# Eight of 18 pairs by seven products in the second pass of the last product, held transposes, and five rooms for the gate2 loads

## The chip, the cores and the metric

The kernel runs on one core of a Trainium2 chip. The core has engines that run side by side, each through its own instructions in a fixed order: TensorE (PE) multiplies matrices into PSUM banks, VectorE (DVE) and ScalarE (ACT) work element by element, GpSimd (POOL) does little here, and SyncE (SP) issues the transfers (DMA) from the chip's memory. An instruction waits until what it reads is written and what it overwrites has been read, and everything behind it on its engine waits with it. The metric is the time of one execution on the device, in microseconds (us).

## The reference, cut to what matters

One layer of a decoder on 256 rows of width 2048: a modulated norm, three token mixers in parallel (stick-breaking attention, dilated attention, gated linear attention) between one input product and one output product, then a modulated norm and a gated feed-forward network of width 5632.

```python
mod = jax.nn.silu(c) @ w_ada[l] + b_ada[l]
shift1, scale1, gate1, shift2, scale2, gate2 = jnp.split(mod[:, None, :], N_MOD, axis=-1)
h = rms_norm(x, norm1_gain[l]) * (1 + scale1) + shift1
x = x + gate1 * mixing_sublayer(h, w_in[l], ...)
h = rms_norm(x, norm2_gain[l]) * (1 + scale2) + shift2
gate, up = jnp.split(h @ w_ffn_in, 2, axis=-1)
x = x + gate2 * ((jax.nn.silu(gate) * up) @ w_ffn_out)
```

Everything is float32. In the mixers, queries and keys are normalised head by head before the attentions.

## The kernel before, in words

**Products.** Rows lie in two tiles of 128 (t = 0, 1), weights come in loads of two chunks of 128 rows by 512 columns (512 KB, the tile `raw`, issued by SP: L146 in `load_weights`, L1293 in `load_pair`). Each load is split into a high and a low part: ACT casts it (`whi`, L158 and L1305) and DVE subtracts (`wlo`, L159 and L1306). There are four buffers of each. A product is three matmuls of 512 columns (`mm3`, L164 to L166): high by high, high by low, low by high. `block` runs the plain loop over the chunks; at given steps it calls other work, and a small counter (`tick`) hands out background work at a set rate.

**Seven products for eight.** `fast_products` multiplies a pair of chunks by a pair of column blocks and a pair of row tiles. A plain pair takes 8 products, 24 matmuls. A fast pair takes 7 products, 21 matmuls, on sums of the weights' quarters (four DVE subtractions of 128x512, L1309, and two further splits from the tiles `AR0` and `AR1`) and on sums of the activations' quarters made beforehand (`sums_of_h2`, `sums_of_unit`). Four extra banks collect shared products, which DVE merges after the last fast pair (L1381 to L1384, L1340). `load_pair` is called three pairs ahead where there are hooks, for all pairs at once where there are none; its instructions have priority for the scheduler that orders each engine.

**The feed-forward part.** The input product runs over 11 units of 512 columns; units 1 to 7 by fast pairs, units 8 to 10 plainly. Each unit's activation (hi, lo) stays in SBUF as four chunks, 44 in all, which are 22 pairs for the last product: unit e holds pairs 2e and 2e+1. The last product makes output blocks 0 and 1 in a first pass over all 22 pairs (`OUT_A`, 6 fast) and blocks 2 and 3 in a second pass over the first 14 pairs (`OUT_B`, 6 fast: 8 to 13, from units 4, 5 and 6); the other 8 pairs are then done for block 2 (a `block` over chunks 28 to 43) and for block 3 (28 and 29 with both row tiles, the rest first for row tile 0, then for row tile 1, with weights of the last 14 chunks kept, three pairs of loads of them in the tiles H2 to H7). `add_out` multiplies by gate2, adds to x2 and stores (L1447, L1449).

**Sums for the last product.** `sums_of_unit` adds hi and lo (L1462), makes four sums (L1269), casts (L1466) and subtracts (L1467). It is hooked to pairs 2, 4 and 6 of OUT_A; its results stay in H2 to H7.

**gate2.** While units 8 to 10 run, 32 loads of w_ada (512 KB each, L384) come into a ring of three tiles, `AR0`, `AR1`, `KC`, and DVE accumulates them into `ada` (L289). The loads stand on SP's queue among the weight loads. After OUT_A's fast pairs, `parts_of_gate2` and `rows_of_gate2` turn the sums into rows with a few matmuls.

**x2.** The four blocks of the first residual (A2, A3, A4, A8) are put away in memory during the feed-forward part, where their tiles serve as further rooms for split weights in units 1 to 7, and brought back (`bring_back`) by hooks at pairs 8 to 11 of OUT_A.

**Mixers.** After the input blocks 0 to 5, `qk_turn(sb_parts, ...)` transposes normalised queries and keys of the stick-breaking heads with PE (L658) into `misc` banks, and ACT copies them back scaled (L659), which frees the bank. `gla()` follows with 32 small matmuls (L734, L738) and then its own blocks, with steps of the stick-breaking attention among them. For the dilated heads, `qk_norm` squares (L638, ACT), takes a reciprocal root (L269 to L277, DVE and ACT) and multiplies (L646, DVE); `dil_steps` then puts two turns and two halves of the scores (L882, L883) at steps 4, 7, 10 and 13 of the second row block. The softmax across groups uses L898 to L924 (L906 is its Exp on ACT), and PE transposes the weights at L936. The gate blocks copy their result out (L1054), and the sigmoids of the gates come at L1071 and L1074.

**Order.** No order is written out by hand. A scheduler orders each engine's instructions by priority and by readiness in its own model; `prio()` raises priority, and `issue_after` holds an instruction behind a given matmul. A change in one place therefore can move instructions in others.

Of the kernel before, what the change touches and what calls it, by code (L numbers as in the profile page):

```python
# [11 lines left out]
F32R = mybir.dt.float32r  # L12
# [5 lines left out]
P = 128  # L18
T = 256
NT = T // P  # L20
D = 2048
KC = D // P
DFF = 5632
NB = 512
# [20 lines left out]
FAST = range(1, 8)  # L45
OUT_UNITS = (4, 5, 6)
OUT_A = tuple((p, 0) for p in range(8)) + tuple(x for i in range(6) for x in ((8 + i, 1), (14 + i, 0))) + ((20, 0), (21, 0))
OUT_B = ((0, 0), (1, 0)) + tuple(x for i in range(6) for x in ((8 + i, 1), (2 + i, 0)))
PAIRS = ((0, 0), (1, 0), (5, 1), (2, 0), (6, 1), (7, 1), (3, 0), (4, 0))
# [26 lines left out]
def trunk(ctx: ExitStack, tc: tile.TileContext, I, out):  # L76
# [16 lines left out]
    def S(tag, shape, dtype=F32):  # L93
        return slot.tile(shape, dtype, tag=tag, name=nm(tag))
# [22 lines left out]
    state = {"rate": 0.0}  # L117
# [358 lines left out]
    LAST = len(GROUPS) - 1  # L476
# [245 lines left out]
    def gla():  # L722
# [21 lines left out]
        for i, b in enumerate((9, 10, 11, 12)):  # L744
            proj_block(LAST, b, steps={1: lambda: sb_step(2 * i), 3: lambda: sb_step(2 * i + 1)})
        with tc.issue_after(state["mm"].ins), prio():
# [268 lines left out]
    proj_block(LAST, 5)  # L1015
    qk_turn(sb_parts, state["mm"].ins)
    sb_hi, sb_lo, sb_step = stick_breaking()
    og = gla()
    for b in range(6, 9):
# [7 lines left out]
    dil_steps = {  # L1027
        4: lambda: qk_turn(dil_parts[:2]),
        7: lambda: qk_turn(dil_parts[2:]),
        10: lambda: dil_scores(0, 3),  # L1030
        13: lambda: dil_scores(3, 6),
    }
# [185 lines left out]

    def bring_back(n):
        x2[n] = S(X2_TAGS[n], [P, NT, NB])  # L1220
        nc.sync.dma_start(x2[n], x2_away[n])
# [176 lines left out]
    for i in range(NFF):  # L1398
        if i in FAST:
            pg, pu = fast_unit(i)  # L1400
        else:
            pg = [acc_bank() for _ in range(NT)]
        if i == FAST[-1] + 1:
            bg.append(gate2_bg())
        if i in FAST:
# [47 lines left out]
    KF = 4 * NFF  # L1453
    CUT = KF - 14
    w_fo = I["w_ffn_out"]
    out_sums = {}

    def sums_of_unit(n):

        e = OUT_UNITS[n]  # L1460
        full = S("AR0", [P, 4, T])
        nc.vector.tensor_tensor(full, act[e][0].bitcast(F32), act[e][1].bitcast(F32), op=ALU.add)  # L1462
        sf = S("AR1", [P, 4, 2, P])
        sums_of(sf, [full[:, :, t * P : (t + 1) * P] for t in range(NT)], slice(0, 4, 2), slice(1, 4, 2))
        hi, lo = (S(f"H{2 + 2 * n + i}", [P, 4, 2, P], F32R) for i in range(2))
        nc.scalar.copy(hi, sf)  # L1466
        nc.vector.tensor_tensor(lo, sf, hi.bitcast(F32), op=ALU.subtract)  # L1467
        for m in range(2):
            out_sums[2 * e + m] = [(hi[:, j, m, :], lo[:, j, m, :]) for j in range(4)]
# [26 lines left out]

    for n in range(4):
        hooks[8 + n] = lambda n=n: bring_back(n)
    behind = 1 + max(n for n, (_, fast) in enumerate(OUT_A) if fast)
    assert behind + 2 < len(OUT_A)  # L1500
    hooks[behind] = lambda: parts_of_gate2(0)
    hooks[behind + 1] = lambda: both(0)
    hooks[behind + 2] = lambda: rows_of_gate2(1)
    o = fast_products(w_fo, 0, NB, OUT_A, act_at, out_sums, acc_bank, misc_bank, ("AR0", "AR1"), hooks)
# [5 lines left out]
    o = fast_products(w_fo, 2 * NB, 3 * NB, OUT_B, act_at, out_sums, misc_bank, acc_bank, ("AR0", "AR1"), more=True)  # L1510
    REST = 2 * len(OUT_B)
    block(o[0], act_at, w_fo, REST, KF, 2 * NB, go_on=True, seeded=True)
# [4 lines left out]
    n, pss = 3, o[1]  # L1517
    block(pss, act_at, w_fo, REST, CUT, n * NB, go_on=True, more=True, seeded=True)
    w = load_weights(w_fo, CUT, KF, n * NB, spare=[f"H{j}" for j in range(2, 8)])
    block(pss, act_at, None, CUT, KF, 0, w=w, tiles=(0,), go_on=True, seeded=True)  # L1520
# [40 lines left out]
```

## Time and profile before

| | us |
|---|---|
| median of three runs | 1593.85 |
| the three runs | 1590.32, 1593.85, 1594.32 |
| the profiled execution | 1593.15 |
| its span | 1591.4 |
| last matmul starts | 1587.0 |
| PE busy | 1576.3 |
| DVE busy | 1299.3 |
| ACT busy | 850.2 |
| bytes moved by DMA | 400.16 MB |

The span is the time between the first and the last recorded instruction; the execution's own time is 1.75 us longer. A row of a timeline has the start, the duration, engine, line, operation, output and input, and in square brackets how long the engine stood idle before it and what ended that wait. Matmuls are pipelined: each lasts longer than the distance to the next start, so gaps of PE are seen in the starts. Times in the kernel's lines are those of the kernel before; the changed kernel's lines are up to four higher.

### The profile page before, as it was taken

What the parts mean: (1) busy time and instruction counts of PE and PEld (TensorE: products, weight loads), DVE (VectorE), ACT (ScalarE), POOL (GpSimd) and SP (SyncE); (2) the same over time, 40 slices, a digit from 0 to 9 for tenths busy, and PEclk for the clock granted to TensorE, in tenths of its full rate; (3) what the DMA queues carried; (4) which work ended last, traced back from release to release, by engine and by line L of the source; (5) the groups of instructions that cost most, each with busy time, mean ns of one, the idle gap of its engine ahead of it and who ended that gap; (6) DMA issues with size and microseconds to landing.
All of it is one profiled execution on the core that took longest, in us unless ns stands there. A gap on an engine that the chain in (4) does not pass through costs nothing.

```text
span 1591.4 us, 20176 instructions
## 1 busy us (share of the span) xinstructions
PE 1576.3 (99%) x7243; PEld 1304.6 (82%) x7243; DVE 1299.3 (82%) x1556; ACT 850.2 (53%) x1193; POOL 11.2 (1%) x22
## 2 busy tenths in 40 slices
PE   8999999999999999999999999999999999999998
PEld 7878888888788888888887888888888888888887
DVE  6889996888888686877756689999997777989884
ACT  5654448775755444444445755555554444455552
POOL 1000000000000000000000000000000000000000
PEclk9999999999999999999999999999999999999999
DMA  9999997667788899988767556666668889756664
GB/s 330 357 331 322 332 305 235 220 193 248 233 273 271 297 306 316 317 283 293 230 210 240 179 185 196 194 202 196 211 189 276 283 294 313 244 185 218 205 206 139
DMA packets 195740, 400.16 MB, mean 251 GB/s; under 512 B 13038, under 2 KB 28052, under 8 KB 195640
## 3 DMA queue, kind: packets, MB, share of 16 engines
q1 hardware_dynamic: 194664, 396.70, 75.6%
q0 software_dynamic: 800, 2.11, 0.3%
q8 instruction: 57, 0.93, 0.3%
q14 instruction: 43, 0.35, 0.1%
q10 hardware_dynamic: 176, 0.07, 0.0%
HBM read 394.63 MB, written 4.19 MB: 251 GB/s over the span
## 4 chain that ended last, share of the span: by engine, by line
PE 86%; DMA 5%; DVE 5%; ACT 3%; issue 1%; SPq 0%; ACTq 0%; DVEq 0%
PE acc L166 21%; PE acc L165 21%; PE acc L164 21%; PE misc L165 6%; PE misc L166 6%; PE misc L164 6%; DMA raw<-w_ffn_out 1%; DMA AR<-w_ada 1%; DVE ada L289 1%; ACT whi L158 1%; DVE wlo L159 1%; PE misc L809 1%; DMA A<-w_ada 1%; DMA OS<-w_ada 1%; DVE wlo L1306 1%
## 5 line engine op out<-in xcount | busy, mean ns | idle before, releaser
L158 ACT CAST whi<-raw 128x1024 fp32r<-128x1024 f32 x362 | 368.6, 1022 | 411.0 <-PE acc L166 257.2
L159 DVE TENSOR_TENSOR wlo<-raw,whi 128x1024 fp32r<-128x1024 f32 x362 | 426.2, 1184 | 181.3 <-ACT whi L158 179.0
L164 PE MATMUL acc<-whi,H 128*128 128x512 f32 x1245 | 487.3, 392 | 1.4 <-ACT H L455 0.8
L165 PE MATMUL acc<-wlo,H 128*128 128x512 f32 x1245 | 486.5, 391 | 0.8 <-DVE wlo L159 0.7
L166 PE MATMUL acc<-whi,H 128*128 128x512 f32 x1245 | 485.2, 390 | 0.4 <-DVE H L462 0.4
L166 PEld LDWEIGHTS acc<-whi,H 128*128 128x128 f32 x1245 | 233.5, 188 | 50.6 <-DVE H L462 1.6
L164 PEld LDWEIGHTS acc<-whi,H 128*128 128x128 f32 x1245 | 233.7, 188 | 50.2 <-ACT H L455 1.3
L165 PEld LDWEIGHTS acc<-wlo,H 128*128 128x128 f32 x1245 | 233.8, 188 | 48.7 <-DVE wlo L159 1.7
L1305 ACT CAST whi<-raw 128x1024 fp32r<-128x1024 f32 (+1 forms) x148 | 141.9, 974 | 99.8 <-PE acc L166 40.1
L1306 DVE TENSOR_TENSOR wlo<-raw,whi 128x1024 fp32r<-128x1024 f32 (+1 forms) x148 | 162.6, 1122 | 8.1 <-ACT whi L1305 6.8
L164 PE MATMUL acc<-whi,A 128*128 128x512 f32 x222 | 87.0, 392 | 1.0 <-DVE scr L1429 1.0
L165 PE MATMUL acc<-wlo,A 128*128 128x512 f32 x222 | 86.4, 389 | 0.0
L166 PE MATMUL acc<-whi,A 128*128 128x512 f32 x216 | 84.1, 389 | 0.0
L289 DVE SCALAR_TENSOR_TENSOR ada<-AR,csil,ada 128x1024 f32<-128x1024 f32 x60 | 76.1, 1280 | 7.3 <-DMA AR<-w_ada 7.3
L165 PE MATMUL misc<-wlo,H 128*128 128x512 f32 x158 | 61.7, 390 | 0.8 <-DVE wlo L1306 0.8
L164 PE MATMUL misc<-whi,H 128*128 128x512 f32 x158 | 61.7, 391 | 0.0
L166 PE MATMUL misc<-whi,H 128*128 128x512 f32 x158 | 61.5, 389 | 0.0
L164 PEld LDWEIGHTS acc<-whi,A 128*128 128x128 f32 x222 | 41.7, 188 | 9.8 <-issue 1.4
L165 PEld LDWEIGHTS acc<-wlo,A 128*128 128x128 f32 x222 | 41.7, 188 | 8.6 <-DVE wlo L159 0.2
L1305 ACT CAST whi<-AR 128x1024 fp32r<-128x1024 f32 x24 | 25.3, 1053 | 43.6 <-PE acc L166 21.1
L1305 ACT CAST A<-raw 128x1024 fp32r<-128x1024 f32 (+1 forms) x36 | 34.9, 982 | 25.0 <-PE misc L166 8.6
L166 PEld LDWEIGHTS acc<-whi,A 128*128 128x128 f32 x216 | 40.5, 188 | 8.5
(485 smaller groups left out, 2291.0 us busy)
## 6 DMA issues: line engine op xcount, KB each, us to landing
raw<-w_in SPq DMA_DIRECT2D x205, 512.0 KB, 5.2
raw<-w_ffn_in SPq DMA_DIRECT2D x176, 512.0 KB, 4.5
raw<-w_ffn_out SPq DMA_DIRECT2D x88, 512.0 KB, 4.9
AR<-w_ada SPq DMA_DIRECT2D x79, 512.0 KB, 5.0
raw<-w_out SPq DMA_DIRECT2D x32, 512.0 KB, 4.9
KC<-w_ada SPq DMA_DIRECT2D x30, 512.0 KB, 5.2
OS<-w_ada SPq DMA_DIRECT2D x16, 512.0 KB, 6.9
KD<-w_ada SPq DMA_DIRECT2D x16, 512.0 KB, 5.5
```

Of the source, the lines that this page charges most:

```text
L158: state["cast"] = nc.scalar.copy(hi[:, :n, :], raw[:, :n, :])
L159: state["split"] = nc.vector.tensor_tensor(lo[:, :n, :], raw[:, :n, :], hi[:, :n, :].bitcast(F32), op=ALU.subtract)
L164: nc.tensor.matmul(ps, lh, rh, start=start, stop=False, skip_group_check=seeded)
L165: nc.tensor.matmul(ps, lh, rl, start=False, stop=False, skip_group_check=seeded)
L166: state["mm"] = nc.tensor.matmul(ps, ll, rh, start=False, stop=stop, skip_group_check=seeded)
L289: nc.vector.scalar_tensor_tensor(acc, raw, c, acc, op0=ALU.mult, op1=ALU.add)
L809: nc.tensor.matmul(ps[:n, t * N_GLA + h, :].rearrange("p (s l) -> p s l", l=L), at(f, h, t)[:, :n], odd(at(f, h, t)), start=True, stop=True,)
L1305: nc.scalar.copy(hi[:, :n, :], src)
L1306: state["split"] = nc.vector.tensor_tensor(lo[:, :n, :], src, hi[:, :n, :].bitcast(F32), op=ALU.subtract)
```

## The change

The second pass goes over 18 pairs instead of 14, eight of them fast: pairs 6 and 7 (unit 3) join, and a fourth call of `sums_of_unit` makes their sums into A4 and A8, hooked to the pair behind the second `rows_of_gate2`. The rest of block 2 is then 8 chunks instead of 16. Block 3's rest is the same 8 chunks, all of them kept for the second row tile, without the spare rooms H2 to H7. The ring of gate2 gets A2 and A3 as fourth and fifth tiles from unit 8 on. Two blocks of x2 come back in OUT_A as before, the other two after OUT_B's code, into H2 and H3. In the mixers, the first two stick-breaking parts are turned where all four were, and the other two at step 2 of the first block inside `gla`. The dilated turns and scores move from steps 4, 7, 10, 13 to 7, 10, 13, 15, and the turns are held behind the matmul before their step.

```diff
-OUT_UNITS = (4, 5, 6)
+OUT_UNITS = (4, 5, 6, 3)
-OUT_B = ((0, 0), (1, 0)) + tuple(x for i in range(6) for x in ((8 + i, 1), (2 + i, 0)))
+OUT_B = ((0, 0), (1, 0)) + tuple(x for a, b in zip((8, 9, 10, 11, 12, 13, 6, 7), (2, 3, 4, 5, 14, 15, 16, 17)) for x in ((a, 1), (b, 0)))
...
-            proj_block(LAST, b, steps={1: lambda: sb_step(2 * i), 3: lambda: sb_step(2 * i + 1)})
+            steps = {1: lambda: sb_step(2 * i), 3: lambda: sb_step(2 * i + 1)}
+            if i == 0:
+                steps[2] = lambda: qk_turn(sb_parts[2:], state["mm"].ins)
+            proj_block(LAST, b, steps=steps)
...
-    qk_turn(sb_parts, state["mm"].ins)
+    qk_turn(sb_parts[:2], state["mm"].ins)
...
-        4: lambda: qk_turn(dil_parts[:2]),
-        7: lambda: qk_turn(dil_parts[2:]),
-        10: lambda: dil_scores(0, 3),
-        13: lambda: dil_scores(3, 6),
+        7: lambda: qk_turn(dil_parts[:2], state["mm"].ins),
+        10: lambda: qk_turn(dil_parts[2:], state["mm"].ins),
+        13: lambda: dil_scores(0, 3),
+        15: lambda: dil_scores(3, 6),
...
-    def bring_back(n):
-        x2[n] = S(X2_TAGS[n], [P, NT, NB])
+    def bring_back(n, tag):
+        x2[n] = S(tag, [P, NT, NB])
...
         if i == FAST[-1] + 1:
+            ring["tags"] = ("AR0", "AR1", "KC", "A2", "A3")
             bg.append(gate2_bg())
...
-    CUT = KF - 14
+    CUT = 2 * len(OUT_B)
...
-        hi, lo = (S(f"H{2 + 2 * n + i}", [P, 4, 2, P], F32R) for i in range(2))
+        hi, lo = (S(tag, [P, 4, 2, P], F32R) for tag in (("H2", "H3"), ("H4", "H5"), ("H6", "H7"), ("A4", "A8"))[n])
...
-    for n in range(4):
-        hooks[8 + n] = lambda n=n: bring_back(n)
+    for n in range(2):
+        hooks[8 + n] = lambda n=n: bring_back(n, X2_TAGS[n])
...
-    hooks[behind + 2] = lambda: rows_of_gate2(1)
+    hooks[behind + 2] = lambda: (rows_of_gate2(1), sums_of_unit(3))
...
     o = fast_products(w_fo, 2 * NB, 3 * NB, OUT_B, act_at, out_sums, misc_bank, acc_bank, ("AR0", "AR1"), more=True)
-    REST = 2 * len(OUT_B)
+    for n in (2, 3):
+        bring_back(n, f"H{n}")
+    REST = CUT
...
-    block(pss, act_at, w_fo, REST, CUT, n * NB, go_on=True, more=True, seeded=True)
-    w = load_weights(w_fo, CUT, KF, n * NB, spare=[f"H{j}" for j in range(2, 8)])
+    w = load_weights(w_fo, CUT, KF, n * NB)
```

## The prediction, made before the changed kernel was run

> **What bounds the kernel now.** I read the profile from its summary inwards: busy time, then PE's total of waits, then the pace of PE in quiet stretches, then a timeline around each gap.
>
> ```profile
> span 1591.4 us, 20176 instructions
> PE 1576.3 (99%) x7243; PEld 1304.6 (82%) x7243; DVE 1299.3 (82%) x1556; ACT 850.2 (53%) x1193; POOL 11.2 (1%) x22
> ...
> L158 ACT CAST whi<-raw 128x1024 fp32r<-128x1024 f32 x362 | 368.6, 1022 | 411.0 <-PE acc L166 257.2
> ```
>
> The only engine without room is PE. ACT's casts wait mostly for PE to free a buffer (257.2 of 411.0 us), not for data. So two things shorten the run: fewer matmuls, or fewer gaps between them. A window in a quiet stretch (busy time and count by engine, granted clock, DMA share, GB/s) gives the pace:
>
> ```profile
> 1160.00:1200.00 40.00, 40.00 (x182) 33.21 (x181) 37.31 (x47) 22.08 (x26) 0.00 (x0) 1.00 0.65 205
> ```
>
> With the clock at 1.00, matmuls of 512 columns start every 0.2267 us (40 us hold some 176 of them and a few shorter ones; 1352.67 and 1352.90 below are two such starts). "Excess" below means a start-to-start distance less its normal one. The list of PE's waits (in all, times, longest) names the longest two that bear on this change:
>
> ```profile
> PE misc L658 <- DVE A L646: 1.8, 2, 1.1
> PE acc L164 <- DVE scr L1429: 1.0, 1, 1.0
> ```
>
> With those that the timelines below show, the gaps that this change can remove add up to some 5.5 us of 1591.
>
> **Fewer matmuls.** In OUT_B a fast pair and a plain pair are 21 + 24 matmuls. Two more fast pairs take 3 each from the program, and the instruction orders agree: PE has 7077 instructions before and 7071 after. 6 x 0.2267 = **-1.36 us**, if DVE and ACT can feed it. The steady cycle in OUT_B:
>
> ```profile
> 1498.55 0.68 DVE L1309 TENSOR_TENSOR AR<-raw,raw 128x512 f32<-128x512 f32 x1
> ...
> 1503.97 1.22 DVE L1306 TENSOR_TENSOR wlo<-AR,whi 128x1024 fp32r<-128x1024 f32 x1 [1.07 <-ACT whi L1305]
> ...
> 1508.75 0.69 DVE L1309 TENSOR_TENSOR AR<-raw,raw 128x512 f32<-128x512 f32 x1
> ```
>
> One cycle is 10.20 us, 45 matmuls, and DVE idles 1.07 of it waiting for a cast that itself waits for a freed buffer. Two more such cycles therefore run at PE's pace. The start of OUT_B is another matter: the sums of a fourth unit (L1462, four L1269, L1467) now stand in DVE's order between the split of the first fast pair's half tile and its subtractions. Groups between 1352 and 1400 us give their price:
>
> ```profile
> L1467 DVE TENSOR_TENSOR H<-AR,H 128x1024 fp32r<-128x1024 f32 x3 | 3.7, 1217 | 0.0
> L1269 DVE TENSOR_TENSOR AR<-AR,AR 128x256 f32<-128x256 f32 x6 | 2.5, 419 | 0.1
> ...
> L1462 DVE TENSOR_TENSOR AR<-A,T 128x1024 f32<-128x1024 f32 x1 | 1.2, 1216 | 0.0
> ```
>
> 1.22 + 4 x 0.42 + 1.22 = 4.1 us, a little less when the four overlap. Before, this is where DVE stood:
>
> ```profile
> 1474.39 2.36 DVE L1306 TENSOR_TENSOR wlo<-raw,whi 128x1024 fp32r<-128x1024 f32 x2
> ...
> 1478.47 1.42 DVE L1309 TENSOR_TENSOR AR<-raw,AR 128x512 f32<-128x512 f32 x2
> 1481.14 1.22 DVE L1306 TENSOR_TENSOR wlo<-AR,whi 128x1024 fp32r<-128x1024 f32 x1 [1.26 <-ACT whi L1305]
> ```
>
> Stepping DVE on from 1476.7 with these durations, the second split of a sum ends at 1486.7; PE, counted on at 0.2267, wants it at 1486.4. I take **+0.4 us** (with 0.1 for the semaphore), between 0 (DVE's order finishes earlier) and 1.5 (the whole 4.1 less the two idle times of 1.26 per pair). The next pair starts with DVE about level, and 1.07 us of idle per cycle takes up the rest. The last blocks lose their six spare rooms: counting on from the last OUT_B matmul, the four loads of block 3 can start 1 us before to 4.4 us after it, their last split waits for DVE's additions of block 2 and ends 14.5 us after it, and PE wants it at 15.2: no gap.
>
> **Gate2 loads.** Their ring grows from three rooms to five from unit 8 on, and x2 comes back later, two of four blocks in OUT_B. The gap they caused:
>
> ```profile
> 1348.32 1.22 DVE L1306 TENSOR_TENSOR wlo<-raw,whi 128x1024 fp32r<-128x1024 f32 x1
> 1351.08 1.29 DVE L289 SCALAR_TENSOR_TENSOR ada<-AR,csil,ada 128x1024 f32<-128x1024 f32 x1 [1.54 <-DMA AR<-w_ada]
> 1352.28 1.22 DVE L1306 TENSOR_TENSOR wlo<-raw,whi 128x1024 fp32r<-128x1024 f32 x1
> 1353.42 1.28 DVE L1429 TENSOR_TENSOR scr<-scr,acc 128x512 f32<-128x512 f32 x2
> ...
> 1352.67 0.39 PE L165 MATMUL acc<-wlo,A 128*128 128x512 f32 x1
> 1352.90 0.39 PE L166 MATMUL acc<-whi,A 128*128 128x512 f32 x1
> 1354.25 0.47 PE L164 MATMUL acc<-whi,A 128*128 128x512 f32 x1 [0.96 <-DVE scr L1429]
> ```
>
> PE's excess is 1.35 - 0.23 = 1.12, plus 0.08 in the next start. After the change the L289 ahead of L1429's split reads a tile asked for two rooms earlier, so DVE goes on at 1349.5, and L1429 starts at about 1351.8, before PE's demand at 1353.1: **-1.2 us**. What is late next is the cast of the following load, wanted well behind. The returning blocks of H2 and H3 stand on SP's queue in OUT_B behind the matmuls that last read those tiles; the weight load behind each waits for a split of the pair after that, which ends later. They cost nothing while that holds.
>
> **An order in DVE.** The first fast pair of OUT_A:
>
> ```profile
> 1398.73 0.69 DVE L1309 TENSOR_TENSOR AR<-raw,raw 128x512 f32<-128x512 f32 x1 [2.82 <-DMA raw<-w_ffn_out]
> 1399.34 1.22 DVE L1306 TENSOR_TENSOR wlo<-AR,whi 128x1024 fp32r<-128x1024 f32 x1
> ...
> 1399.47 0.39 PE L164 MATMUL misc<-whi,H 128*128 128x512 f32 x1
> 1400.61 0.50 PE L165 MATMUL misc<-wlo,H 128*128 128x512 f32 x1 [0.76 <-DVE wlo L1306]
> ```
>
> A split that PE needs stands behind a subtraction of the next pair that waits 2.82 us for its load. In the new order the split comes first, and the subtraction three splits later. Excess 0.91 + 0.11: **-1.0 us**.
>
> **Held transposes, dilated.** They leave steps 4/7 for 7/10, held to a matmul; PE meets the first 19 matmuls later.
>
> ```profile
> 414.62 0.76 DVE L646 TENSOR_TENSOR A<-A,tiny 128x256 f32<-128x256 f32 x2
> 417.30 1.29 DVE L646 TENSOR_TENSOR A<-A,tiny 128x512 f32<-128x512 f32 x2
> ...
> 413.62 0.39 PE L166 MATMUL acc<-whi,H 128*128 128x512 f32 x1
> 415.10 0.44 PE L658 MATMUL misc<-ident,A 128*128 128x128 f32 x2 [1.10 <-DVE A L646]
> ...
> 415.08 1.05 ACT L158 CAST whi<-raw 128x1024 fp32r<-128x1024 f32 x1 [1.35 <-DMA raw<-w_in]
> ```
>
> The gap shown is 1.48 - 0.23 = 1.26, and PE's waits on L646 add to it a second of 0.7; with what stands around it, 2.2 in all. But DVE and ACT are reordered too: a cast and a split of a load that landed at 415.0 now stand ahead of the chain that ends in L646. L646 then ends its first tile near 418.6, where PE asks at 418.2, and by the same stepping the next demands are missed by 0.1 to 0.3 each and the score matmuls once by 0.7, behind a split and an L289. Left are 1.0 to 2.0; I take 1.4: **-0.8 us**. Bounds: -2.2 (no gap) and +1.5 (each later tile late by one more split of 1.22).
>
> **Held transposes, stick-breaking.** Four of the eight move past the small matmuls.
>
> ```profile
> 276.73 0.39 PE L166 MATMUL acc<-whi,H 128*128 128x512 f32 x1
> 278.06 1.24 PE L658 MATMUL misc<-ident,A 128*128 128x128 f32 x8 [0.94 <-ACT A L659]
> ...
> 277.32 1.84 ACT L659 ACTIVATE A<-misc,qgains 128x512 f32<-128x512 f32 x3
> ```
>
> What PE reaches instead needs a bank that the same first L659 frees (about 277.9), so most of the 1.1 stays: **-0.25 us**, from 0 to -1.1.
>
> **Two table loads.** The Exp of L906 falls behind the gate's sigmoid, and the function tables are loaded twice more.
>
> ```profile
> 438.51 0.21 ACT L906 ACTIVATE tiny<-tiny 128x12 f32<-128x12 f32 x1
> ...
> 441.67 1.28 ACT L1071 ACT_TABLE_LOAD   x1
> 442.96 1.06 ACT L1071 ACTIVATE A<-A 128x1024 f32<-128x1024 f32 x1
> ...
> 443.99 2.84 DVE L924 TENSOR_SCALAR T<-T,dcoef 128x128 f32<-128x128 f32 x12
> ...
> 445.36 1.50 PE L936 MATMUL misc<-ident,T 128*128 128x128 f32 x9
> ```
>
> Exp then ends near 445.45 instead of 438.7, and L924 begins near 447.8; the transposes that read it (L936) come 11 matmuls later, at 447.85, and want the first of its tiles at 448.05: **+0.2 us**, from 0 to 1.5 (a further table load). The second load stands before gates that no matmul is near.
>
> The Trainium skill, page "ScalarE: Activation LUTs", section "What ACT_TABLE_LOAD costs", adds a drain of about 1.38 us to each switch, 2.66 us in all. This trace disagrees as far as it shows: the activation starts 1.29 us after the load does. By the page's rule L936 would wait 1.4 us longer, and the sum below would be 1590.5.
>
> **Sum.** -1.36 + 0.4 - 1.2 - 1.0 - 0.8 - 0.25 + 0.2 = -4.0 us. The profiled run took 1593.15, its span 1591.4 and 1.75 around it; that is 0.7 under the median of the three runs, which spread over 4 us. 1593.15 - 4.0 = **1589.1 us**.
>
> **Rivals.** *More is freed*: dilated transposes, the stick-breaking ones and the start of OUT_B end without a gap: -1.36 - 1.2 - 1.0 - 2.2 - 1.1 + 0.2 = -6.7, so 1586.5. For it speaks that PE asks 2 to 4 us later; against it the casts now ahead. *The gaps only move*: the transposes gain nothing, the table load costs its 1.5 and OUT_B's start its 1.5, so -1.36 - 1.2 - 1.0 + 3.0 = -0.6: 1592.6. DVE, full for 37 of 40 us in the window at 1160, speaks for it; the slack found step by step speaks against. *Slower*: the five-room ring asks for gate2 tiles (some 30 loads of 512 KB in units 8 to 10 and OUT_A) so early that they go ahead of weight loads. In the window at 1160, 205 GB/s at a share of 0.65 make 315 GB/s when full, so one takes 1.66 us; a cast's average wait on PE, 257.2/362 = 0.71 us, is what hides it, and past that point each costs 0.95. Four in ten hitting, 12 loads, give +11.4: 1600.5. Against it: the same loads are made before, three in a row too. *It does not do what it says* for the matmuls is excluded by the counts.
>
> **From cases to numbers.** About 0.3%, 4.8 us here, can be told from no change; against the median the limits are 1589.1 and 1598.6. The forecast (1587.6 to 1590.6) gets 0.50, cut in half by the limit. More freed: 0.15, faster. Gaps move (1590.6 to 1595): 0.23, same. Slower: 0.12. Faster 0.40, same 0.48, slower 0.12. The range 1586.2 to 1595 leaves out the slower rival and some 0.05 below.
>
> **What would show it.** Right: PE's waits no longer name L1429, nor an L1306 at the start of OUT_A; L658's waits sum to 1 to 2 us; a wait of some 0.4 at OUT_B's first fast pair, and two table loads of 1.28 with Exp right behind. Wrong: casts in units 8 to 10 that wait for DMA, a PE wait in the last two blocks, or L936 waiting over 1 us.

## The result and the profile after

The changed kernel takes 1590.93 us (median of 20 runs, 1588.98 to 1593.55); the kernel before, measured beside it, 1593.39 us (20 runs, 1590.32 to 1596.32). The ratio is 0.9981, with a 95% interval of 0.9975 to 0.9987: 2.1 to 4.0 us, about 0.2%, less. Forecast were 1589.1 us and "same" (0.48) before "faster" (0.40); the change stayed under the 0.3% that was set as the bound.

The page of the changed kernel begins:

```profile
span 1588.5 us, 20191 instructions
...
PE 1576.5 (99%) x7237; PEld 1303.0 (82%) x7237; DVE 1311.0 (83%) x1574; ACT 856.1 (54%) x1200; POOL 11.6 (1%) x22
```

Six matmul records fewer than before, as counted, and 2.9 us less span. Its profiled execution took 1590.29 us. PE's waits in it (total, times, longest):

```profile
PE acc L165 <- DVE wlo L159: 1.4, 2, 0.8
...
PE acc L164 <- ACT whi L1308: 0.5, 1, 0.5
...
PE misc L165 <- DVE wlo L1309: 0.3, 1, 0.3
PE misc L939 <- DVE T L927: 0.2, 1, 0.2
PE misc L164 <- ACT whi L1308: 0.2, 1, 0.2
```

The waits for L1429 and on L646 are gone. New are a second wait on L159, and two waits on casts of L1308. The second wait on L159 is for a load that lands late in the first y block. PE's timeline there:

```profile
572.69 0.50 PE L164 MATMUL acc<-whi,A 128*128 128x512 f32 x1
573.95 0.50 PE L165 MATMUL acc<-wlo,A 128*128 128x512 f32 x1 [0.76 <-DVE wlo L159]
```

and ACT's:

```profile
571.58 1.05 ACT L158 CAST whi<-raw 128x1024 fp32r<-128x1024 f32 x1 [5.02 <-DMA raw<-w_br_gla]
```

ACT had stood idle for 5.02 us when the load came and the cast started at 571.58; the split behind it ended 1.03 us after PE asked (1.26 between starts, 0.23 normal). By then the mixers had freed PE's path: where the prediction showed 1.26 us of gap in the dilated chain, DVE now reads

```profile
414.94 1.23 DVE L159 TENSOR_TENSOR wlo<-raw,whi 128x1024 fp32r<-128x1024 f32 x1 [1.36 <-ACT whi L158]
...
416.94 1.36 DVE L646 TENSOR_TENSOR A<-A,tiny 128x256 f32<-128x256 f32 x3
```

and PE

```profile
417.42 0.78 PE L658 MATMUL misc<-ident,A 128*128 128x128 f32 x4
```

L646 starts at 416.94, and its three tiles are done one by one; PE transposes the first at 417.42 without waiting for DVE. The fourth unit's sums stand in front of what the second pass's first fast pair needs. DVE:

```profile
1473.71 1.22 DVE L1466 TENSOR_TENSOR AR<-A,A 128x1024 f32<-128x1024 f32 x1
...
1475.44 0.75 DVE L1272 TENSOR_TENSOR AR<-AR 128x256 f32<-128x256 f32 x2
1476.12 0.87 DVE L1272 TENSOR_TENSOR AR<-AR,AR 128x256 f32<-128x256 f32 x2
...
1478.24 1.22 DVE L1471 TENSOR_TENSOR A<-AR,A 128x1024 fp32r<-128x1024 f32 x1
1479.52 1.23 DVE L1309 TENSOR_TENSOR wlo<-AR,whi 128x1024 fp32r<-128x1024 f32 x1
1480.66 1.41 DVE L1312 TENSOR_TENSOR AR<-raw,AR 128x512 f32<-128x512 f32 x2
1483.26 1.23 DVE L1309 TENSOR_TENSOR wlo<-AR,whi 128x1024 fp32r<-128x1024 f32 x1 [1.19 <-ACT whi L1308]
```

ACT:

```profile
1482.18 1.05 ACT L1308 CAST whi<-AR 128x1024 fp32r<-128x1024 f32 x1 [2.70 <-DVE AR L1312]
1483.13 1.99 ACT L1308 CAST whi<-raw 128x1024 fp32r<-128x1024 f32 x2
```

PE:

```profile
1482.44 0.39 PE L166 MATMUL acc<-whi,H 128*128 128x512 f32 x1
1483.28 0.50 PE L164 MATMUL acc<-whi,H 128*128 128x512 f32 x1 [0.45 <-ACT whi L1308]
1483.62 0.40 PE L164 MATMUL misc<-whi,A 128*128 128x512 f32 x1
1484.23 0.49 PE L164 MATMUL misc<-whi,A 128*128 128x512 f32 x1 [0.22 <-ACT whi L1308]
1484.57 0.47 PE L165 MATMUL acc<-wlo,H 128*128 128x512 f32 x1
```

The sums push the subtractions (L1312) back, so the cast of their result starts at 1482.18 only. PE asked for it at 1482.67 (the start at 1482.44 and 0.23) and starts at 1483.28, 0.61 us late. The next cast on ACT had to wait its turn and costs 0.39 more. With starts of 0.33 instead of 0.23 behind each wait, 1.3 us are lost here: the gain of the six matmuls.

Over all matmuls, the excess of PE's starts in the trace sums to 1.7 us less after than before. With the 1.36 of six matmuls this makes 3.0, the time from PE's first start to its last, and the span is 2.9 us shorter.

### The profile page after: what moved, and what is told of

Its sections match the earlier page's. It is cut to its first block, busy times and chain, and to the rows that moved or that the text cites. A ratio compares the mean times of both kernels' runs of the same rounds, so it can differ in the third digit from the quotient of the medians.

```text
span 1588.5 us, 20191 instructions
## 1 busy us (share of the span) xinstructions
PE 1576.5 (99%) x7237; PEld 1303.0 (82%) x7237; DVE 1311.0 (83%) x1574; ACT 856.1 (54%) x1200; POOL 11.6 (1%) x22
## 4 chain that ended last, share of the span: by engine, by line
PE 86%; DVE 5%; DMA 4%; ACT 3%; issue 2%; SPq 0%; ACTq 0%; DVEq 0%
PE acc L166 21%; PE acc L165 21%; PE acc L164 21%; PE misc L165 5%; PE misc L166 5%; PE misc L164 5%; DVE wlo L1309 1%; DMA raw<-w_ffn_out 1%; ACT whi L158 1%; DVE wlo L159 1%; DMA raw<-w_br_gla 1%; PE acc L443 1%; DMA raw<-w_ffn_in 1%; PE misc L812 1%; DVE ada L289 1%
## 5 line engine op out<-in xcount | busy, mean ns | idle before, releaser
L158 ACT CAST whi<-raw 128x1024 fp32r<-128x1024 f32 x357 | 363.1, 1021 | 398.5 <-PE acc L166 253.1
L159 DVE TENSOR_TENSOR wlo<-raw,whi 128x1024 fp32r<-128x1024 f32 x357 | 419.4, 1182 | 180.4 <-ACT whi L158 178.4
L1308 ACT CAST whi<-raw 128x1024 fp32r<-128x1024 f32 (+1 forms) x156 | 149.1, 972 | 102.6 <-PE acc L166 32.0
L1309 DVE TENSOR_TENSOR wlo<-raw,whi 128x1024 fp32r<-128x1024 f32 (+1 forms) x156 | 171.0, 1119 | 11.0 <-ACT whi L1308 9.9
L165 PE MATMUL acc<-wlo,A 128*128 128x512 f32 x230 | 89.6, 390 | 0.8 <-DVE wlo L159 0.8
L164 PE MATMUL acc<-whi,A 128*128 128x512 f32 x230 | 90.1, 392 | 0.0
L166 PE MATMUL acc<-whi,A 128*128 128x512 f32 x224 | 87.2, 389 | 0.0
L289 DVE SCALAR_TENSOR_TENSOR ada<-AR,csil,ada 128x1024 f32<-128x1024 f32 x51 | 64.8, 1278 | 2.1 <-DMA AR<-w_ada 2.0
L165 PE MATMUL misc<-wlo,H 128*128 128x512 f32 (+1 forms) x166 | 64.4, 388 | 0.3 <-DVE wlo L1309 0.3
L164 PE MATMUL misc<-whi,H 128*128 128x512 f32 (+1 forms) x166 | 64.4, 388 | 0.0
L166 PE MATMUL misc<-whi,H 128*128 128x512 f32 (+1 forms) x166 | 64.2, 387 | 0.0
L1308 ACT CAST whi<-AR 128x1024 fp32r<-128x1024 f32 x28 | 29.5, 1053 | 45.5 <-DVE AR L1312 22.1
L1308 ACT CAST A<-raw 128x1024 fp32r<-128x1024 f32 (+1 forms) x36 | 34.9, 982 | 26.0 <-DMA raw<-w_ffn_in 11.8
```

What stands on the lines that cost most here:

```text
L158: state["cast"] = nc.scalar.copy(hi[:, :n, :], raw[:, :n, :])
L159: state["split"] = nc.vector.tensor_tensor(lo[:, :n, :], raw[:, :n, :], hi[:, :n, :].bitcast(F32), op=ALU.subtract)
L164: nc.tensor.matmul(ps, lh, rh, start=start, stop=False, skip_group_check=seeded)
L165: nc.tensor.matmul(ps, lh, rl, start=False, stop=False, skip_group_check=seeded)
L166: state["mm"] = nc.tensor.matmul(ps, ll, rh, start=False, stop=stop, skip_group_check=seeded)
L289: nc.vector.scalar_tensor_tensor(acc, raw, c, acc, op0=ALU.mult, op1=ALU.add)
```

## The experiments

All runs below were timed in turns with the kernel before, on one chip per group; the column "kernel before" has its median in that group. The ratio is an estimate from the runs and not the quotient of the two medians; the two differ by up to 1.5 us (sums_unit8). Three segments of PE's time are read from the timelines: from the end of its wait on L462 (near 91 us) to the last L947 of the mixers (L950 in changed code, near 458), from there to the first transpose of gate1's part of norm 2 (L1196 or L1199, near 868), and from there to the last matmul.

| kernel | median, us | kernel before | ratio, 95% interval | 91 to mixers' end | to 868 | to the end |
|---|---|---|---|---|---|---|
| before, first profile | 1593.39 | | | 368.4 | 409.3 | 718.0 |
| before_p1 | 1593.66 | 1593.55 | 1.0001, 0.9991 to 1.0012 | 368.5 | 410.0 | 718.5 |
| changed, first profile | 1590.93 | 1593.39 | 0.9981, 0.9975 to 0.9987 | 366.4 | 410.5 | 716.4 |
| after_p2 | 1590.98 | 1592.78 | 0.9990, 0.9981 to 0.9998 | 366.6 | 409.2 | 717.8 |
| front_only | 1593.54 | 1594.24 | 0.9996, 0.9986 to 1.0006 | 366.5 | 410.4 | 716.4 |
| rooms_only | 1591.68 | 1594.24 | 0.9984, 0.9973 to 0.9995 | 366.9 | 409.8 | 716.5 |
| outb_only | 1594.25 | 1594.24 | 1.0006, 0.9996 to 1.0016 | 367.2 | 409.6 | 719.8 |
| no_front | 1591.64 | 1593.55 | 0.9988, 0.9978 to 0.9997 | 365.8 | 409.8 | 716.6 |
| sums_early | 1595.93 | 1594.24 | 1.0007, 0.9998 to 1.0015 | 366.6 | 410.4 | 722.0 |
| sums_spread | 1592.38 | 1593.55 | 0.9995, 0.9986 to 1.0004 | 367.9 | 410.5 | 717.1 |
| sums_unit8 | 1589.65 | 1592.78 | 0.9971, 0.9959 to 0.9983 | 367.4 | 410.4 | 714.8 |
| ada_later | 1598.00 | 1593.55 | 1.0034, 1.0021 to 1.0046 | 367.7 | 417.6 | 717.2 |
| ada_earlier | 1591.81 | 1592.78 | 0.9993, 0.9985 to 1.0002 | 367.0 | 409.4 | 718.3 |
| both_best | 1588.68 | 1592.78 | 0.9974, 0.9965 to 0.9983 | 366.9 | 409.2 | 715.5 |

**front_only.** The kernel before with the two mixer edits.

```diff
-    qk_turn(sb_parts, state["mm"].ins)
+    qk_turn(sb_parts[:2], state["mm"].ins)
...
+                steps[2] = lambda: qk_turn(sb_parts[2:], state["mm"].ins)
...
-        4: lambda: qk_turn(dil_parts[:2]),
+        7: lambda: qk_turn(dil_parts[:2], state["mm"].ins),
```

> The kernel before with the two held-transpose edits alone (stick-breaking and dilated). Theory A (freed time is handed back where loads bind): PE is 2.0 to 2.5 us ahead of before once the gate blocks begin (near 490 us), but only 1.0 to 1.5 us ahead after the first y block (near 590 us), because a load of w_br_gla lands no earlier; median 1.0 to 1.5 us under before. Theory B (the gap near 573 us in the changed kernel was chance): no such gap, PE stays 2.0 to 2.5 us ahead to the end and the median is 2 us or more under before. The rival of the prediction, that these edits free only 0.85 us, would show a lead under 1.2 us already near 490 us.

The median lies 0.7 us under before, with an interval that includes no change. By the profile, counted from 91 us and against the first profile of before, the lead is 1.9 us at the mixers' end (366.5 against 368.4) and 0.8 at 868, after a gap of 0.95 us near 573. That is theory A in this execution, a little smaller than it said. But this profile also has no gap at 1352 and 1399 us, though nothing was edited there, so single profiles vary there by more than the edits bring.

**rooms_only.** The kernel before with five rooms.

```diff
         if i == FAST[-1] + 1:
+            ring["tags"] = ("AR0", "AR1", "KC", "A2", "A3")
             bg.append(gate2_bg())
```

> The kernel before with the five-room ring for gate2 alone. Theory A: the gap of 1.1 us at the start of the last product (PE waits for L1429) is gone, and the waits of casts for data in units 8 to 10 are as before: 1.2 us less PE time between 1330 and 1370 us, median 1.0 to 1.4 us under before; the gap at the first fast pair of OUT_A stays or shrinks by its order of instructions. Rival (gate2 tiles crowd the weight loads): PE waits for splits or casts appear in units 8 to 10 and the median is level or above before.

As theory A: the wait for L1429 is gone, no wait on a cast or a split appears in units 8 to 10, and the median is 2.6 us lower (interval of the ratio 0.8 to 4.3 us), as much as the whole change gives. That this is more than the 1.1 us gap of the first profile has its reason in the next profiles of three-room kernels.

**outb_only.** The changed kernel with mixers and ring put back, so the second pass alone.

```diff
-            ring["tags"] = ("AR0", "AR1", "KC", "A2", "A3")
...
-    qk_turn(sb_parts[:2], state["mm"].ins)
+    qk_turn(sb_parts, state["mm"].ins)
```

> The changed kernel with both mixer edits and the ring undone: only the 18 pairs with eight fast, the fourth unit's sums and the later return of x2. Theory A: six matmuls less give 1.36 us, the fourth unit's sums on DVE at the start of the second pass take about 1.3 us of it back as two or three gaps of PE near its first fast pair: median within 0.8 us of before. Rival (prediction's size): the gaps there are 0.4 us, median about 1 us under before.

Level with before. Six matmuls less and nothing gained: the gaps at the first fast pair are there again, 0.60 and 0.39 us, the same as in the changed kernel. Its list of waits shows also what three rooms can cost:

```profile
PE misc L165 <- DVE wlo L1306: 1.6, 1, 1.6
...
PE acc L164 <- DVE scr L1429: 1.3, 1, 1.3
```

**sums_early.** The fourth unit's sums at pair 0 of the first pass.

```diff
-for n, at in enumerate((2, 4, 6))}
+for n, at in enumerate((2, 4, 6, 0))}
...
-    hooks[behind + 2] = lambda: (rows_of_gate2(1), sums_of_unit(3))
+    hooks[behind + 2] = lambda: rows_of_gate2(1)
```

> The changed kernel with the fourth unit's sums hooked to pair 0 of the first pass instead of behind the second rows of gate2. Theory A (these sums alone make the gaps at the first fast pair of the second pass): the 1.3 us of gaps near 1483 us are gone, nothing comes back in the first pass beyond 0.3 us, and the median is 1.0 to 1.5 us under the changed kernel's 1590.9, so 1589.4 to 1589.9. Rival (DVE's backlog there has other sources, gate2's rows and the stores): at least 0.6 us of gaps stay near 1483 us and the median is above 1590.3. Rival 2: the sums at pair 0 delay what the first fast pair of the first pass needs, and a gap of 1 us or more appears near 1396 us.

Theory A falls and the second rival holds, larger than it said. DVE ahead of the first pass's first fast pair:

```profile
1391.02 1.22 DVE L1466 TENSOR_TENSOR AR<-T,T 128x1024 f32<-128x1024 f32 x1
...
1396.21 0.68 DVE L1312 TENSOR_TENSOR AR<-raw 128x512 f32<-128x512 f32 x1
```

and PE:

```profile
1395.93 0.39 PE L166 MATMUL acc<-whi,H 128*128 128x512 f32 x1
1398.10 0.73 PE L164 MATMUL misc<-whi,H 128*128 128x512 f32 x2 [1.78 <-ACT whi L1308]
```

All four units' sums go through AR0 and AR1, which the gate2 ring uses as well (its last accumulation from them starts at 1366.88). One unit more in that line pushes the last unit's sums (L1466 at 1391.02) onto the fast pair's subtractions, which use the same two tiles. PE lost 4.7 us between 1395 and 1404 us in gaps of 0.3 to 1.9. The gaps near 1483 us are gone here too.

**before_p1.** The kernel before, unchanged.

> The kernel before once more, unchanged, for a second profile. Theory A (gaps that end in a DMA wait differ from execution to execution, and the stretch near 573 us ties PE to the weight loads whatever came before): the gaps at 1352 and 1399 us, 1.1 and 0.9 us in the first profile, come out different by 0.5 us or more, as do those of the dilated transposes; PE's time at 868 us is within 0.4 us of 867.2, which four other kernels with and without the mixer edits showed. Rival (gaps are fixed by the order of instructions): both repeat within 0.2 us, and PE is at 868.4 again.

The gaps at 1352 and 1399 us have 0.74 and 1.77 us of excess here, 1.13 and 0.92 in the first profile: one is smaller by 0.4 (under the 0.5 said), one larger by 0.85. On DVE both end in a wait for a load:

```profile
1351.16 1.29 DVE L289 SCALAR_TENSOR_TENSOR ada<-AR,csil,ada 128x1024 f32<-128x1024 f32 x1 [1.25 <-DMA AR<-w_ada]
...
1399.65 0.69 DVE L1309 TENSOR_TENSOR AR<-raw,raw 128x512 f32<-128x512 f32 x1 [3.68 <-DMA raw<-w_ffn_out]
```

The first profile had 1.54 and 2.82 in these brackets. The same program's loads land up to 0.9 us earlier or later from one execution to the next, and PE's gap follows. PE reached 868 us later than said too, after a gap of 0.38 near 575 which the first profile does not have. So a gap behind a late load is known from one profile only to about a microsecond, and the sum of the prediction, made against one execution, took several such gaps as fixed.

**no_front.** The changed kernel with the mixers put back.

```diff
-        7: lambda: qk_turn(dil_parts[:2], state["mm"].ins),
+        4: lambda: qk_turn(dil_parts[:2]),
...
-    qk_turn(sb_parts[:2], state["mm"].ins)
+    qk_turn(sb_parts, state["mm"].ins)
```

> The changed kernel with both mixer edits undone, ring and second pass as changed. Theory A: the mixer edits bring nothing to the end, since loads near 573 us set PE's pace there; median within 0.7 us of the changed kernel (1590.2 to 1591.6). Rival (what the mixer edits free reaches the end): 2 us or more above the changed kernel, about 1593.

The median is 1.9 us under before (changed: 2.5 in its own comparison, 1.8 as after_p2), so the mixer edits cannot be told from nothing at the end. The profile shows why the gaps in the mixers are no fixed quantity either:

```profile
PE misc L248 <- DMA A<-x: 2.2, 1, 2.2
...
PE misc L658 <- DVE A L646: 0.2, 1, 0.2
```

In this execution PE lost 2.2 us at the start, and the old order of the transposes lost 0.39 us of excess on L646 where the first profile of before lost 2.1. The first segment is the shortest of all, 365.8, without the edits. A later PE finds more loads landed; that this is the whole reason was not tried.

**sums_spread.** The changed kernel with the fourth unit's sums cut into four pieces, hooked to pairs of the first pass, in scratch tiles of their own.

```diff
-        hooks[8 + n] = lambda n=n: bring_back(n, X2_TAGS[n])
+    hooks[8] = lambda: bring_back(0, X2_TAGS[0])
+    hooks[16] = lambda: bring_back(1, X2_TAGS[1])
...
+    hooks[9] = spread_full
+    hooks[11] = lambda: spread_sums(0)
+    hooks[13] = lambda: spread_sums(1)
+    hooks[15] = spread_split
```

> The changed kernel with the fourth unit's sums in four pieces, at the plain pairs 9, 11, 13 and 15 of the first pass (scratch in KC and A3; x2's second block comes back at pair 16). Theory A (4.1 us of DVE work in one place makes the 1.3 us of gaps at the second pass's first fast pair, and there is 1.07 us of idle in each cycle to take a piece): no gap over 0.25 us near 1483 us, none new between 1400 and 1450 us, median 0.8 to 1.4 us under the changed kernel: 1589.5 to 1590.1. Rival (any further DVE work between fast pairs delays them, too): gaps of 0.3 us or more follow the pieces, and the median is level with the changed kernel.

The gap at the second pass's start is gone: no start between 1465 us and the end has over 0.25 us of excess. But the first pass has 0.57, 0.49 and 0.38 between 1396 and 1400 us, where the changed kernel's first profile has one gap of 0.47, and 0.42 near 1462 (a gap there is seen in other kernels too, see after_p2), and the median is not under the changed kernel's. The rival, that pieces among the fast pairs delay those, holds in part.

**ada_later.** The changed kernel with fewer loads of w_ada in the stretch before 573 us, and more behind it.

```diff
     for br in range(3):
+        if br == 2:
+            state["rate"] = 0.3
         gate_block(1, br)
     y_block(0)
+    state["rate"] = 0.8
     for br in range(3):
         gate_block(2, br)
+    state["rate"] = RATE_MID
```

> The changed kernel with the background rate of the w_ada loads cut from 0.6 to 0.3 in the third gate block of the second column and the first y block, and raised to 0.8 in the three gate blocks behind. Theory A (near 573 us the weight loads land late because DMA is full, a share of 0.9 and more, and PE's lead from the mixer edits is lost there): the wait on the split near 573 us is gone or under 0.3 us, PE stands 0.8 us or more further ahead at 868 us (866.4 or less), and the median is 0.5 to 1.2 us under the changed kernel. Rival (the wait comes from the order of SP's queue or of DVE, not from the amount of data): the gap stays within 0.3 us of 1.0. Rival 2: the gap is gone, but the loads that were put off make another in the gate blocks behind, and 867.2 stays.

The gap near 573 is gone, and the median is 4.5 us above the kernel before, 7 above the changed kernel's in the other groups: the loads put off meet the next block's, and the stretch to 868 us takes 417.6 instead of 410.5. The window of 600 to 670 us (busy time and count by engine, clock, DMA share, GB/s):

```profile
600.00:670.00 70.00, 64.77 (x285) 52.32 (x283) 50.72 (x50) 27.84 (x34) 0.00 (x0) 1.00 0.91 314
```

and at its end ACT

```profile
667.67 1.04 ACT L158 CAST whi<-raw 128x1024 fp32r<-128x1024 f32 x1 [7.48 <-DMA raw<-w_br_gla]
```

With a share of 0.91 over 70 us, a load issued at 659.77 comes just before its cast starts at 667.67, and PE stands idle 3.0 us for that cast. The second rival holds, by far larger than it said. It fits theory A that the gap near 573 is gone, but one profile does not show the cause: the changed kernel's second profile, with nothing edited, has no gap there either, and the share between 548 and 573 us is 0.92 in its first profile, 0.94 in its second and 0.92 in the first of before, which has none.

**sums_unit8.** The changed kernel with the fourth unit's sums made once, before the five-room ring opens at unit 8, in A2 and A3, which are free there.

```diff
+    def sums_of_unit3():
+        full = S("A2", [P, 4, T])
+        nc.vector.tensor_tensor(full, act[3][0].bitcast(F32), act[3][1].bitcast(F32), op=ALU.add)
+        sf = S("A3", [P, 4, 2, P])
...
+        hi, lo = (S(tag, [P, 4, 2, P], F32R) for tag in ("A4", "A8"))
...
         if i == FAST[-1] + 1:
+            sums_of_unit3()
             ring["tags"] = ("AR0", "AR1", "KC", "A2", "A3")
...
-    hooks[behind + 2] = lambda: (rows_of_gate2(1), sums_of_unit(3))
+    hooks[behind + 2] = lambda: rows_of_gate2(1)
```

> The changed kernel with the fourth unit's sums made at the start of unit 8 of the input product (scratch in A2 and A3 before they join the gate2 ring), where DVE has room, and nothing at the second pass. Theory A (the sums cost PE only where fast pairs leave DVE no room): the gaps of 0.6 and 0.4 us near 1483 us are gone and no gap over 0.3 us is new; PE's time from 868 us to its last matmul is 715.6 to 716.2 us instead of 717.0; median 0.7 to 1.3 us under the changed kernel in the same call. Rival (the pieces displace gate2's accumulation and the gap at L1429 comes back): a gap of 0.5 us or more near 1352 us, no gain.

The median is 1589.65, 1.3 us under the changed kernel in the same group and 3.1 under before. DVE at the second pass's first fast pair:

```profile
1478.69 1.22 DVE L1309 TENSOR_TENSOR wlo<-AR,whi 128x1024 fp32r<-128x1024 f32 x1 [0.97 <-ACT whi L1308]
1481.41 1.23 DVE L1309 TENSOR_TENSOR wlo<-AR,whi 128x1024 fp32r<-128x1024 f32 x1 [1.50 <-ACT whi L1308]
```

PE around the demands that were late in the changed kernel:

```profile
1482.57 0.39 PE L166 MATMUL acc<-whi,H 128*128 128x512 f32 x1
1482.80 0.39 PE L164 MATMUL acc<-whi,H 128*128 128x512 f32 x1
...
1483.93 0.39 PE L166 MATMUL acc<-whi,H 128*128 128x512 f32 x1
1484.16 0.39 PE L164 MATMUL misc<-whi,A 128*128 128x512 f32 x1
```

DVE idles twice where it was busy with sums, and PE starts every 0.23 us with no wait on L1308. The segment to the end is 714.8, against 716.4 and 717.8 of the two profiles of the changed kernel, but not all of that is the edit. A gap near 873 us, 0.65 and 0.57 in those two and behind a cast that waits for a load, is 0.1 here, although the engines' order is the same up to 1212 us; and one of 0.72 stands near 1460 us, against the theory's "no gap over 0.3 us is new" (it is the gap of after_p2 below). The times are the better evidence: the 1.3 us read as a loss in the changed kernel's trace come back as 1.3 us of median, and of eleven runs three are over the fastest of the changed kernel's eleven. The intervals of the two ratios (0.9959 to 0.9983 and 0.9981 to 0.9998) overlap by a little.

**ada_earlier.** The changed kernel with more loads of w_ada in the first gate blocks, and fewer in the stretch before 573 us.

```diff
+    state["rate"] = 0.75
     gate_block(0, 0)
...
     for br in range(3):
+        if br:
+            state["rate"] = RATE_MID if br == 1 else 0.3
         gate_block(1, br)
     y_block(0)
+    state["rate"] = RATE_MID
```

> The changed kernel with the background rate of the w_ada loads raised from 0.6 to 0.75 in the three gate blocks of the first column and cut to 0.3 in the third gate block of the second column and the first y block; 4.8 steps move forward, none back. Theory A (amount of data near 573 us): the wait on the split near 573 us, 1.0 us in the changed kernel, falls under 0.3, nothing new comes before it, and PE's time from 90 to 868 us falls from 777.1 to 776.5 or less. Rival (the loads cannot be moved without paying: the stretches around are full as well): a gap of 0.5 us or more at another place between 425 and 870 us and 777 or more.

The casts near 573 us wait for PE again:

```profile
570.84 1.06 ACT L158 CAST whi<-raw 128x1024 fp32r<-128x1024 f32 x1 [1.66 <-PE acc L166]
```

No gap is left there, and none of ada_later's losses appear. From 91 to 868 us it takes 776.4, the changed kernel 776.9 and 775.8; the median is 1591.81 against 1590.98. No gain is shown.

**both_best.** The edits of sums_unit8 and ada_earlier together.

> The changed kernel with the sums at unit 8 and the w_ada loads earlier, both. Theory A: the two add up; median 1.3 us or more under the changed kernel in the same call, so under before by 3.8 us or more. Rival: one of them is paid back, median within 0.7 us of the changed kernel.

1588.68 us: 2.3 under the changed kernel in the same group, 4.1 under before (the ratio's interval gives 2.7 to 5.6), the best median here. Its interval overlaps that of sums_unit8, so what the second edit adds is open.

**after_p2.** The changed kernel, unchanged.

> The changed kernel once more, unchanged, for a second profile and as the yardstick of this call. Theory A: the gaps near 1483 us (0.6 and 0.4, casts that wait for DVE) repeat within 0.1 us, being fixed by the order of work; the gap near 573 us and what the mixers show differ by more, since they end in loads; no gap over 0.3 us near 1352 us. Rival (the ring only had luck in its first profile): a gap of 0.5 us or more near 1352 us. Median 1.8 to 3.2 us under before.

The two gaps at the second pass's first fast pair have 0.62 and 0.39 us, in the first profile 0.61 and 0.39. Those behind loads moved: there is no gap at 573 or at 1395 us, and a new one of 1.0 at 1457.7. None stands near 1352 us. ACT and DVE near 1457 us, in two fences:

```profile
1455.97 1.05 ACT L1308 CAST whi<-raw 128x1024 fp32r<-128x1024 f32 x1 [2.73 <-DMA raw<-w_ffn_out]
```

```profile
1457.05 1.23 DVE L1309 TENSOR_TENSOR wlo<-raw,whi 128x1024 fp32r<-128x1024 f32 x1 [1.33 <-ACT whi L1308]
1458.19 0.69 DVE L1343 TENSOR_TENSOR acc<-acc,KC 128x512 f32<-128x512 f32 x1
```

The merge's addition (L1343), which needs no load, stands behind a split that waits for one. This gap is 0 to 1.3 us in the profiles here: none in before, before_p1, rooms_only, sums_early, ada_later and the first profile of the changed kernel, 0.42 to 0.50 in front_only, outb_only, no_front and sums_spread, 0.72 in sums_unit8, 0.94 in both_best, 1.28 in ada_earlier. Whether the change makes it likelier is open.

## Why the prediction was partly right

The forecast of 1589.1 lies 1.8 us under the measured 1590.93, which is in the range and among the cases called "same". By the time alone it falls 0.3 us inside the band given to the rival *the gaps only move*; by its causes it is the forecast with one term too small and others that hold only in some executions. Term by term, with the excess read from the profiles:

| term | forecast | changed, its two profiles | profiles without the edit |
|---|---|---|---|
| six matmuls | -1.36 | -1.36 | |
| start of OUT_B | +0.4 | 1.3 and 1.3 lost | none lost |
| gate2 rooms | -1.2 | none left, none left | 1.13, 0.74, 1.46, 0 lost |
| order in DVE | -1.0 | 0.47 left, none left | 0.92, 1.77, 1.76, 0 lost |
| dilated transposes | -0.8 | none left, none left | 2.1, 1.5, 1.8, 0.8, 0.4 lost |
| stick-breaking | -0.25 | 0.35 left, 0.22 left | 1.10, 0.91, 0.26, 0.73, 0.22 lost |
| table loads | +0.2 | +0.15 and +0.15 | |

The last column has before and before_p1 first and outb_only third. In the rows of the rooms and of the order in DVE, front_only is fourth: these two go together, since rooms_only has the new order at the first pass's fast pair. In the rows of the mixers, rooms_only and no_front are fourth and fifth.

Between the first profile of before and that of the changed kernel these terms come to -4.3 us, because the mixers' transposes freed 2.8 there and not 1.05; the gap near 573 us, which the forecast does not have, takes 1.0 of it back, and the span is 2.9 us shorter. That a sum of -4.0 lies so near these -4.3 is in part luck: a price too small at OUT_B stands against a gain too small in the mixers. The six matmuls are six in the traces, too (7243 and 7237 records); no run here shows the totals 7077 and 7071 that the prediction names.

**The step that was mis-sized** is "I take +0.4 us" for the start of OUT_B. The sums took 4.0 us of DVE, as priced at 4.1. But from the first of them to the end of the second split of a sum it took 10.8 us (1473.71 to 1484.49), where the stepping had 10.0 (1476.7 to 1486.7). The rows quoted after the result show what the chain holds behind the sums: the first split of a sum (L1309) ahead of the second pair of subtractions, then the cast (1.05), for which DVE idles 1.19 us, then the split. Before, both pairs of subtractions came ahead of the first of these splits. The stepping is not written out in the prediction, so that this order makes up the 0.8 us is likely, but not shown. With 0.8 more, PE is not only late for that split. It already waits for the cast that the split needs, which was in time by the forecast's numbers (a split of 1.22 that ends at 1486.7 puts that cast's end at 1485.5), and for the cast queued behind that one on ACT. PE reaches the split's matmul 1.2 us late, and loses 1.3 with the slower starts behind the waits. That took the whole gain of the six matmuls: outb_only is level with before, and sums_unit8, without the term, is 1.3 us faster. The upper bound given, 1.5, held.

**Gate2 rooms: right, and by the medians practically the whole gain.** PE waits for L1429 in no profile with five rooms. rooms_only alone is 2.6 us faster than before. The 1.2 of the forecast was the first profile's gap; over the four profiles with three rooms that gap is 0.83 on average. The gap at the first pass's fast pair is 1.11 on average in those four, and 0.23 in the eight with five rooms and no sums added in the first pass (all but sums_early and sums_spread). Together that is 1.7 us, within rooms_only's interval of 0.8 to 4.3.

**Order in DVE: right in kind, half in size.** A split no longer stands behind a subtraction that waits for a load. In the first profile of the changed kernel 0.47 us were left all the same, behind something else: the sums of the last of the first three units and the cast of the subtractions' result. DVE:

```profile
1392.44 1.22 DVE L1471 TENSOR_TENSOR H<-AR,H 128x1024 fp32r<-128x1024 f32 x1
1393.69 1.42 DVE L1312 TENSOR_TENSOR AR<-raw,AR 128x512 f32<-128x512 f32 x2
1395.03 2.50 DVE L1309 TENSOR_TENSOR wlo<-AR,whi 128x1024 fp32r<-128x1024 f32 x2
```

Nothing here waits, DVE is simply full. For the gate2 rooms the forecast asked what is late next; here it did not.

**Held transposes: right on average where they stand, nothing to be seen at the end.** I let a load land at 415.0, as in the profile of before, and put its cast and split ahead of L646. In both profiles of the changed kernel the loads had landed earlier and L646 was in time, so 2.1 us were saved there and not 0.8, and the waits of 1 to 2 us on L658, named as a sign of being right, did not come. In four other edited kernels 0.36 to 1.45 were left (both_best, ada_later, ada_earlier, sums_unit8). The largest has on ACT

```profile
413.38 0.22 ACT L271 ACTIVATE tiny<-tiny 128x24 f32<-128x24 f32 x1 [0.24 <-DVE tiny L269]
414.93 1.05 ACT L158 CAST whi<-raw 128x1024 fp32r<-128x1024 f32 x1 [1.32 <-DMA raw<-w_in]
415.88 0.21 ACT L272 ACTIVATE tiny<-tiny 128x24 f32<-128x24 f32 x1
```

where the changed kernel's first profile has

```profile
413.86 1.05 ACT L158 CAST whi<-raw 128x1024 fp32r<-128x1024 f32 x1
414.81 0.22 ACT L272 ACTIVATE tiny<-tiny 128x24 f32<-128x24 f32 x1
```

The chain that ends in L646 goes through L272, which stands behind a cast; it is late by as much as that cast's load is. Over the nine profiles with the edit the dilated gaps are 0.4 us on average, over the five without it 1.3: the size that was forecast, but as an average, in which a load's landing decides each case.

For the stick-breaking transposes no gain shows: PE still waits on the first L659, as forecast, and over the same profiles the gap is 0.6 us on average with the edit and 0.6 without it, where -0.25 was counted.

To the mixers' end, and behind them, little of this lasts. From 91 us to their end, the profiles without the edits take 367.4 us on average (before, before_p1, rooms_only, outb_only, no_front) and those with them 366.9 (the changed kernel, after_p2, front_only, sums_early, sums_spread, sums_unit8). From 91 to 868 us it is 777.0 and 777.1. By their medians, front_only is 0.7 us under before and no_front as good as the changed kernel. The forecast counted -1.05 for the mixers as if nothing stood behind them. That the lead is lost to the full transfers near 573 us fits the gap of 0.95 to 1.03 us there in the changed kernel's first profile, front_only, sums_spread and sums_unit8; that it is always so was not shown, and ada_earlier, which clears that stretch, gained nothing that shows.

**Table loads: right.** ACT in the changed kernel:

```profile
441.38 1.28 ACT L909 ACT_TABLE_LOAD   x1
442.67 0.21 ACT L909 ACTIVATE tiny<-tiny 128x12 f32<-128x12 f32 x1
```

Exp starts 1.29 us after its load does, and PE waits 0.2 us on L927. The Trainium skill's page "ScalarE: Activation LUTs" (section "What ACT_TABLE_LOAD costs") adds a drain of 1.38 us; no room for it is in these rows, and 1590.5, which the sum would have been by it, came close to the result for another reason.

**The last blocks.** No gap was forecast. The first profile has none; after_p2 has 0.26 us of excess near 1577 and ada_earlier 0.60 near 1578, each a split of a load that PE waits for.

**The slower rival**, gate2 loads ahead of weight loads in units 8 to 10, is refuted: in no profile with five rooms does PE wait for a cast or a split between 1100 and 1390 us by over 0.25. *More freed* was right for the dilated transposes in these two executions and wrong for OUT_B.

## What to carry to other kernels

When DVE's work is moved ahead of a chain, step the whole chain to the last consumer, casts between engines included, and give the end an error of its own: here 0.8 us in 10 made a term three times as large. A gap that ends in a load's landing is an average over executions, so take it from two or three profiles before summing it; a gap that ends in an engine's order can be taken from one. Time freed ahead of a stretch in which the transfers are full counts only once that stretch has been shown to follow.

## What the runs showed of the hardware

Loads of one program land at different times from execution to execution. Gaps behind them varied from 0.92 to 1.77 us (before and before_p1, near 1399 us) and from 0 to 1.0 (the changed kernel, twice, at 573 and 1457 us), while the gap set by DVE's order alone was 0.60 to 0.62 us in five of the six profiles that have the sums there (0.92 in ada_later, where DVE also idled 0.36 us for a cast). The kernel that waited longest for x at its start, no_front with 2.2 us, then took the least time from 91 us to the mixers' end (365.8 us), in the one profile there is of it.
